# Two-layer attention encoder: the transposed blocks of P change places inside SBUF, and the products with v come later

## The chip, the core and the metric

The kernel runs on one core of a Trainium2 chip. The metric is device time in microseconds (us). The engines are TensorE (PE; PEld is its weight load), VectorE (DVE), ScalarE (ACT), GpSimd (POOL) and SyncE (SP), which here issues almost every DMA; DMAs that one engine issues go out in its program's order.

## The reference

Two layers on 512 tokens of width 1024, in float32. Layer A is dilated sliding-window attention (three dilations, merged by their softmax denominators), layer B is neighbourhood attention on an 8 x 64 grid.

```python
def reference(x, ...):
    for i in range(DEPTH):                      # DEPTH = 2
        hn = rms_norm(x, norm_gain[i])
        y = mixer_a(...) if i % 2 == 0 else mixer_b(...)
        x = x + y

def mixer_a(hn, w_in, w_out, q_gain, k_gain, t5_bias):
    qkv, gate = split(hn @ w_in)                # q, k, v for 3 dilations, 16 heads of 64
    for g, (window, dilation) in enumerate(DILATED_PAIRS):
        q, k = rms_norm(q, q_gain[g]), rms_norm(k, k_gain[g])
        o, lse = dilated_group_attention(q, k, v, bias, dilation, reach)
    y = sum(softmax(lses) * outs) * silu(gate)
    return y @ w_out

def mixer_b(hn, w_in, w_out, q_gain, k_gain, rpb):
    q, k, v, gate = split(hn @ w_in, 4)
    q, k = rms_norm(q, q_gain) * HEAD_DIM ** -0.5, rms_norm(k, k_gain)
    p = softmax(q k^T + bias)                   # 8 rows x 16 columns of neighbours
    y = (p v) * silu(gate)
    return y @ w_out
```

## The kernel before

Heads go in pairs: `NHC` = 8 pairs per layer, called heads below. Two generators run against each other and make one program for TensorE, in whose order it runs. `main` holds the dense products: for each head of layer A a projection of 512 columns to `rawk` (raw k and v), one to `rawq` (raw q and k), one to v of the first dilation (`vt`) and one to the gate; for each head of layer B one of 384 columns to `raw` (q, k, v) and one to the gate. A projection to raw takes 8 steps of 12 matmuls, the gate and `vt` 8 steps of 3, because a float32 product is made of three: `wh` with `hn_h`, `wl` with `hn_h` and `wh` with `hn_l` (a weight and an input are each split into a high and a low part).

`side` holds the attention of a head: its norm, transposes of raw q and k on TensorE (`tp`), two pairs of score tiles (`log`), softmax, the transposes of P and the products `o` of P with v (`weigh`), and `put_y`, which multiplies `o` with the gate and splits the result into `y_h` and `y_l` for the output product. After each piece of `main` the function `run` asks whether the next piece of `side` is due. A `yield` of a number in `side` lets so many ns of modelled TensorE work go by; `yield "wait", stamp, n` counts n from the moment when a stamp was set. So the numbers in the diff move pieces of `side` along TensorE's program, and no engine waits for them by time. TensorE's order is kept as it is written; the other engines' orders come from a scheduler.

P is transposed in two steps. VectorE turns each 32x32 block in place (`put`, L615, into tile `tr`); then the blocks have to change places between four groups of 32 partitions. `out` (L617) does that by writing `tr` to DRAM (`td`, L620) and reading it back in four pieces of 32 partitions (L622, into tile `pt`). A batch is one such exchange: two per head in layer A (run 512, 1 MB), one in layer B (run 448, 0.9 MB), for seven of the eight heads; the last head of a layer transposes P on TensorE. There is one `tr` and one `pt`. In layer A `o` follows 19 us of modelled work after the second batch; in layer B, `o` of a head is held in `pending` and made 10 us of work after the next head's projection to raw.

Weights come through SP's queue too, in loads of 512 or 384 KB (`wraw`, L174, three buffers); ScalarE casts them to `wh`, and VectorE or GpSimd makes `wl`, four steps ahead of TensorE. With the raw loads they run some ten steps ahead. Accumulators of projections (`acc`) use four PSUM banks in turn, `tp`, `log` and `o` four others. `gt` and `eg` of the gate have two buffers each. `head_norm` makes the norm's scale `rs`, on VectorE for `rawq` and by a chain of 14 small instructions on GpSimd for `rawk` and layer B's `raw`, and L271 applies it on VectorE.

Of the kernel before, what the change touches and what calls it, by code (L numbers as in the profile page):

```python
# [12 lines left out]
F32 = mybir.dt.float32  # L13
# [8 lines left out]
P = 128  # L22
# [3 lines left out]
NHC = 8  # L26
# [15 lines left out]
def tile_hybrid_encoder(  # L42
# [13 lines left out]
    nc = tc.nc  # L56
# [5 lines left out]
    wk = ctx.enter_context(tc.tile_pool(name="wk", bufs=2))  # L62
    ps_acc = ctx.enter_context(tc.tile_pool(name="ps_acc", bufs=4, space=PSUM))
    ps_side = ctx.enter_context(tc.tile_pool(name="ps_side", bufs=4, space=PSUM))
    dr = ctx.enter_context(tc.tile_pool(name="dr", bufs=1, space=DRAM))
# [326 lines left out]
        nc.sync.dma_start(lb_d, lb)  # L392

    st = {}

    def project_qk(n, ns, key, hc, guard, first=False, **kw):

        box = []

        def evac(i, acc):  # L400
            if not box:
                q = key == "rawq"
                box.append(wk.tile([P, 4, n], F32, tag="rawq" if q else "rawk", name=key, bufs=1 if q else 2))
                box.append(wk.tile([P, 32], F32, tag="ss", name="ss"))
            raw, ss = box
            if first:
                nc.scalar.copy(raw[:, i, :], acc[:, :n])
                return
            nc.scalar.activation(raw[:, i, :], acc[:, :n], AF.Copy, scale=rs_n[:, i : i + 1])  # L409
            squares(raw, ss, i, ns)  # L410

        tile_of = lambda hn: lambda k, i: hn[:, k, P * i : P * (i + 1)]
        yield from project(tile_of(hn_h), tile_of(hn_l), n, evac, guard, **kw)
        raw, ss = box
        if first:
            st["first"] = raw, ss
            return
        normed(raw, ss, ns, key, hc)
# [46 lines left out]
    def k_a(hc):  # L465
        yield "wait", ("rawk", hc), 10000 if hc else 12500
        k12 = wk.tile([P, 2, 512], F32, tag="k12", name="k12", bufs=1)
        raw = st.pop(("rawk", hc))
        for g in range(2):
            tp = transpose4(raw, g * P)  # L470
            nc.vector.tensor_scalar(k12[:, g, :], tp, gk[:, g + 1 : g + 2], None, op0=ALU.mult)
            yield
        st["k12", hc] = k12, raw
        stamp["k12", hc] = 0
# [129 lines left out]
    class turner:  # L604
# [11 lines left out]

        def out(self, dst):  # L617
            run = self.run
            d = dr.tile([P, 4 * run], F32, tag="td", name="td", bufs=2)
            nc.sync.dma_start(d, self.t)  # L620
            for b in range(4):
                nc.sync.dma_start(  # L622
                    dst[32 * b : 32 * b + 32, :].rearrange("p (a x) -> p a x", a=4),
                    bass.AP(d.tensor, d.offset + run * b, [[4 * run, 32], [128 * run, 4], [1, run]]),
                )

    def attn_a(hc):
        e0, e12 = st.pop(("e", hc))
# [2 lines left out]
        pts = []  # L631
# [77 lines left out]
        def weigh():  # L709
            o = bank("o")  # L710
            mms = []
            for g in range(2):
                for j in range(4):
                    c = 256 + P * g
                    mms.append((
                        lambda t_, j=j: sb(t_, 32 * j, [[256, 2], [P, 2], [1, 32]]),
                        lambda hs, j=j, c=c: v12[:, j, c + hs.start : c + hs.stop],
                        lambda hd, g=g, j=j: sb(pts[0], at(0, j, hd, 2 + g), [[2048, 2], [128, 2], [1, 32]]),
                    ))
            for i in range(4):  # L720
                (t0, i0), (t1, i1) = ((i - 1, 1), (i, 0)) if i else ((0, 0), (3, 1))
                mms.append((
                    lambda t_, d=P * t0, n=P * (t1 - t0): sb(t_, d, [[n, 2], [32, 4], [1, 32]]),
                    lambda hs, i=i: v0[hc % 2][:, i, hs],
                    lambda hd, t0=t0, i0=i0, n=at(t1, 0, 0, i1) - at(t0, 0, 0, i0): sb(
                        pts[0], at(t0, 0, hd, i0), [[n, 2], [512, 4], [1, 32]]
                    ),
                ))
            side_by_side(o, mms)
            return o  # L730

        if hc < NHC - 1:
            for u in range(2):
                yield 2500 if u == 0 else 8000
                turned = turner(512)
                for hd, t, pr in scores(u):
                    turned.put(pr, 512, 256 * hd + 128 * (t % 2))
                turned.out(pts[0][:, 2048 * u : 2048 * u + 2048])
            yield 19000
        else:  # L740
            for u in range(2):
                yield 1200
                held = scores(u)
                yield 3200
                for args in held:
                    turn_p(*args)
                    yield
            yield from v_a(hc)
            stamp["ya", "turned"] = 0
        o = weigh()  # L750
        if hc == NHC - 2:
            gap[0] = cycle((500, 500, 700))
            yield "wait", ("gate", hc), 1500
        put_y(hc, o, True, hc == NHC - 1)
        yield

    def run(main, side):

# [29 lines left out]
    gap = [cycle((1200,))]  # L788
# [71 lines left out]
        nc.scalar.activation(eg, gt, AF.Tanh, scale=0.5)  # L860
        gated(hc, gt, eg)

    pending = []

    def side_b(hc):
        if hc:
            yield "wait", ("raw", hc), 10000
            pending.pop()()
            yield 2500 if hc < NHC - 1 else 1000
        else:  # L870
            yield "wait", ("raw", hc), 12000
        raw = st.pop(("raw", hc))
        e = st.pop(("e", hc))
        qh = wk.tile([P, 512], F32R, tag="q0h", name="qh", bufs=1)
# [6 lines left out]
        for src, h, l in (  # L881
# [1 line left out]
            (edge_rc(tp), edge_q(qh), edge_q(ql)),  # L883
        ):
            nc.vector.tensor_sub(l, src, h.bitcast(F32))
        yield 2500
        tp = transpose4(raw, P)
        put_k([(kh, kl, tp)], 3)
        stamp["qk", hc] = 0
        yield 1750  # L890
        pts = []

        at = lambda a, hd, i: 448 * a + 224 * hd + 32 * i

        def scores(u):
            if u == 0:
                pts.append(wk.tile([P, 4096], F32, tag="pt", name="pt", bufs=1))
            lgs = [bank("log") for _ in range(2)]
            for b in (2 * u, 2 * u + 1):
                if b < 3:  # L900
                    m = lambda t_, hs: t_[hs, P * b : P * b + 256]
                else:
                    m = lambda t_, hs: sb(t_[hs], 0, [[384, 2], [1, P]])
                qs = slice(P * b, P * b + P)
                o = 256 * (b % 2)
                mm3_heads(
                    [lg[:, o : o + 256] for lg in lgs],
                    lambda hs: qh[hs, qs], lambda hs: ql[hs, qs], lambda hs: m(kh, hs), lambda hs: m(kl, hs), True,
                )
            return [(hd, u, softmax(hd, u, lgs[hd])) for hd in range(2)]  # L910
# [59 lines left out]
        for u in range(2):  # L970
            held += scores(u)
            yield 1200 if u == 0 else 2400
        if hc < NHC - 1:
            turned = turner(448)
            for hd, u, pr in held:
                turned.put(pr, 512 if u == 0 else 384, 224 * hd + 128 * u)
            turned.out(pts[0][:, :1792])
            pending.append(lambda: put_y(hc, weigh(), False, False))
            return
# [20 lines left out]
    def side():  # L1000
        for k in range(KT):
            norm(0, k, x_all[:, k, :])
            if k:
                square_a(k - 1)
            stamp["na", k] = 0
            yield 1000
        square_a(KT - 1)
        for k in range(1, KT):
            yield 1300
            nc.vector.tensor_add(x_all[:, 0, :], x_all[:, 0, :], x_all[:, k, :])  # L1010
        yield 1500
        row_scale(row_sums(x_all[:, 0, :]))
        st["y_h"] = big.tile([P, KT, S], F32R, tag="y", name="y_h")
        yield 2500
        bias_lines()
        st["e", 0] = bias_a(0)
        yield 2500
        scales_a()
        first_out()
        stamp["rs", "a"] = 0  # L1020
        for hc in range(NHC):
            if hc < NHC - 1:
                yield from chain(k_a(hc), q_a(hc), v_a(hc), attn_a(hc))
                if hc == 2:
                    bias_rows()
            else:
                yield from chain(q_a(hc), k_a(hc), attn_a(hc))
        yield from residual(xg)
        stamp["ya", KT - 1, "y"] = 0
        for f in range(KT):  # L1030
            yield "wait", ("x", f), 2500
            square_b(f)
        yield 1500
        row_scale(row_sums(st.pop("ssq")))
        yield 5000
        nc.scalar.copy(rs_all, spread())
        stamp["rs", "b"] = 0
        for hc in range(NHC):
            yield from side_b(hc)
            if hc + 2 < NHC:  # L1040
                st["e", hc + 2] = bias_b(hc + 2)
        yield from residual(xm_d)
        stamp["yb", KT - 1, "y"] = 0

    run(main(), side())


# [88 lines left out]
```

## Time and profile before

| what | before |
|---|---|
| time, median of three runs | 1015.43 us (1013.43 to 1016.85) |
| the profiled execution | 1015.75 us, span 1014.0 us |
| TensorE busy, mean granted clock | 891.6 us (88%), 0.938 |
| VectorE, ScalarE, GpSimd busy | 505.6 us (50%), 423.7 us (42%), 300.0 us (30%) |
| DMA | 130.48 MB, 129 GB/s over the span |
| HBM read, written | 103.73 MB, 25.75 MB |

The span is that of the core from its first to its last instruction; the execution's own time is measured around it. Busy shares are means over stages with different limits, so an engine far under 100% can still be waited for in one place.

### The profile page before, as it was taken

The page shows a single profiled execution, that of the slowest core. Times are in us where ns is not written, and L with a number is a line of the kernel's source. Part 1 is how long each engine was busy: PE and PEld are TensorE (multiplying, and loading weights), DVE is VectorE, ACT ScalarE, POOL GpSimd, SP SyncE. Part 2 cuts the span into 40 slices and gives each one's busy share as a digit, 9 for nine tenths or more (in the row PEclk, how much of TensorE's full clock was granted, in tenths as well). Part 3 has the DMA queues.
Part 4 walks back from the last instruction along what each step waited for, and adds up shares of the span by engine and source line. Part 5 has one row for each costly group of instructions (what it writes and reads, how often), then busy time and mean ns, then how long its engine had stood idle before and what let it go on. Part 6 is the DMA issues. An engine that isn't in the chain of part 4 may idle for free.

```text
span 1014.0 us, 15414 instructions
## 1 busy us (share of the span) xinstructions
PE 891.6 (88%) x5629; PEld 739.1 (73%) x5629; DVE 505.6 (50%) x1324; ACT 423.7 (42%) x888; POOL 300.0 (30%) x500
## 2 busy tenths in 40 slices
PE   9999799799799899899799899999769588596698
PEld 7787678587678678677687777889658577585476
DVE  6365265366355456366366554546354353362442
ACT  6436235236234425335235444535245253352451
POOL 2342233232341331332332411133332232241311
PEclk9999899999899999999899899999898798797899
DMA  6344613714622723714713613622451442424314
GB/s 231 95 140 140 201 63 126 215 63 140 200 81 96 209 98 118 224 63 127 215 63 128 200 48 97 214 91 78 149 150 38 140 142 61 141 91 126 117 52 177
DMA packets 51787, 130.48 MB, mean 129 GB/s; under 512 B 5504, under 2 KB 20288, under 8 KB 49920
## 3 DMA queue, kind: packets, MB, share of 16 engines
q1 hardware_dynamic: 51424, 129.49, 40.7%
q8 instruction: 44, 0.72, 0.3%
q14 instruction: 31, 0.25, 0.1%
q10 hardware_dynamic: 288, 0.01, 0.0%
HBM read 103.73 MB, written 25.75 MB: 128 GB/s over the span
## 4 chain that ended last, share of the span: by engine, by line
PE 56%; DMA 18%; DVE 12%; ACT 8%; issue 3%; SPq 2%; POOL 1%; ACTq 0%; DVEq 0%; POOLq 0%
PE acc L205 42%; DMA td<-tr 10%; DMA pt<-td 7%; PE o L205 7%; PE tp L209 4%; PE log L205 3%; ACT p L542 2%; SPq L622 2%; DVE wl L130 2%; ACT p L934 2%; DVE tr L615 1%; DVE rawq L271 1%; ACT wh L126 1%; ACT rawk L409 1%; ACT p L698 1%
## 5 line engine op out<-in xcount | busy, mean ns | idle before, releaser
L205 PE MATMUL acc<-wh,hn_h 128*128 128x512 f32 (+1 forms) x768 | 301.6, 393 | 7.0 <-ACT rawk L409 2.1
L126 ACT CAST wh<-wraw 128x512 fp32r<-128x512 f32 (+1 forms) x276 | 161.6, 586 | 309.4 <-PE acc L205 268.2
L205 PE MATMUL acc<-wl,hn_h 128*128 128x512 f32 (+1 forms) x768 | 289.0, 376 | 0.4 <-DVE wl L130 0.4
L205 PE MATMUL acc<-wh,hn_l 128*128 128x512 f32 (+1 forms) x768 | 288.7, 376 | 0.0
L130 POOL TENSOR_TENSOR wl<-wraw,wh 128x512 fp32r<-128x512 f32 (+1 forms) x110 | 138.1, 1255 | 407.9 <-ACT wh L126 368.6
L130 DVE TENSOR_TENSOR wl<-wraw,wh 128x512 fp32r<-128x512 f32 (+1 forms) x166 | 114.2, 688 | 150.2 <-ACT wh L126 145.9
L205 PEld LDWEIGHTS acc<-wh,hn_h 128*128 128x128 f32 x768 | 147.0, 191 | 41.7 <-issue 8.7
L205 PEld LDWEIGHTS acc<-wh,hn_l 128*128 128x128 f32 x768 | 146.6, 191 | 21.4
L205 PEld LDWEIGHTS acc<-wl,hn_h 128*128 128x128 f32 x768 | 147.1, 192 | 18.9 <-DVE wl L130 0.9
L205 PE MATMUL o<-pt,raw 128*64 128x64 f32 (+2 forms) x192 | 24.5, 436 | 66.5 <-DMA pt<-td 66.3
L205 PE MATMUL acc<-hn_h,wh 128*128 128x512 f32 x192 | 76.5, 399 | 0.1
L565 DVE SCALAR_TENSOR_TENSOR gt<-gt,o 128x512 f32<-128x512 f32 x15 | 10.3, 688 | 132.9 <-PE o L205 132.8
L205 PE MATMUL acc<-hn_h,wl 128*128 128x512 f32 x192 | 75.1, 391 | 0.0
L205 PE MATMUL acc<-hn_l,wh 128*128 128x512 f32 x192 | 75.0, 390 | 0.0
L542 ACT ACTIVATE p<-p,mn 128x512 f32<-128x512 f32 (+3 forms) x128 | 70.8, 588 | 1.2 <-DVE mn L541 1.2
L205 PEld LDWEIGHTS o<-pt,raw 128*64 128x64 f32 x192 | 17.3, 214 | 73.5 <-issue 63.2
L698 ACT ACTIVATE p<-p,mn 128x512 f32<-128x512 f32 (+1 forms) x64 | 44.9, 702 | 50.3 <-DVE mn L687 50.3
L205 PE MATMUL o<-pt,rawk 128*64 128x128 f32 x256 | 27.3, 399 | 39.3 <-DMA pt<-td 28.2
L256 POOL TENSOR_TENSOR sq<-rawq 128x512 f32<-128x512 f32 x32 | 33.9, 1072 | 92.1 <-ACT rawq L409 91.4
L615 DVE STREAM_TRANSPOSE tr<-p 128x512 f32<-128x512 f32 (+1 forms) x84 | 55.8, 682 | 9.1 <-ACT p L542 8.5
L257 DVE TENSOR_REDUCE ss<-sq 128x4 f32<-128x256 f32 (+1 forms) x96 | 47.9, 500 | 23.3 <-POOL sq L256 22.9
L205 PEld LDWEIGHTS o<-pt,rawk 128*64 128x64 f32 x256 | 24.7, 213 | 42.5 <-issue 42.5
(137 smaller groups left out, 1253.5 us busy)
## 6 DMA issues: line engine op xcount, KB each, us to landing
wraw<-in_w SPq DMA_DIRECT2D x95, 512.0 KB
wraw<-in_w SPq DMA_DIRECT2D x38, 384.0 KB
td<-tr SPq DMA_DIRECT2D x14, 1024.0 KB
pt<-td SPq DMA_DIRECT2D x56, 256.0 KB
td<-tr SPq DMA_DIRECT2D x7, 896.0 KB
pt<-td SPq DMA_DIRECT2D x28, 224.0 KB
e<-l_d SPq DMA_DIRECT2D x32, 112.0 KB
e<-l_d SPq DMA_DIRECT2D x16, 128.0 KB
```

The costliest lines, as they stand in the source:

```text
L126: nc.scalar.copy(h, raw)
L130: eng.tensor_sub(l, raw, h.bitcast(F32))
L205: nc.tensor.matmul(o, l, r, **kw)
L209: nc.tensor.transpose(o, i, ident)
L256: nc.gpsimd.tensor_mul(sq, raw[:, i, : ns * 64], raw[:, i, : ns * 64])
L257: nc.vector.tensor_reduce(ss[:, i * ns : (i + 1) * ns], sq.rearrange("p (a b) -> p a b", b=64), axis=AX.X, op=ALU.add)
L542: nc.scalar.activation(pr, pr, AF.Copy, scale=mn[:, 3:4])
L565: nc.vector.scalar_tensor_tensor(gt, gt, 0.5, o, op0=ALU.mult, op1=ALU.mult)
L615: nc.vector.transpose(dst, src[:, :n].rearrange("p (i b k) -> p i b k", b=4, k=32))
L622: nc.sync.dma_start(dst[32 * b : 32 * b + 32, :].rearrange("p (a x) -> p a x", a=4), bass.AP(d.tensor, d.offset + run * b, [[4 * run, 32], ...
L698: nc.scalar.activation(row, row, AF.Exp, bias=mn[:, 1:2], scale=-1.0, accum_out=mn[:, 2:3])
L934: nc.scalar.activation(pr[:, o : o + n], pr[:, o : o + n], AF.Exp, bias=mn[:, 0:1], scale=-1.0, accum_out=mn[:, 2:3])
```

## The change

`out` no longer goes through DRAM: 16 DMAs copy block (a, b) of `tr` straight to its place in `pt`, 32 partitions by `run` columns each. In layer A the products with v are held in `pending` and made during the next head, 24 us of modelled work after its projection to `rawk` (in the last head after the transposes of raw q); the second pair of scores comes 12 us of work after the first instead of 8. In layer B `o` of a head is made after the next head's two pairs of scores, not ahead of its transposes. Raw k and v of layer A and raw q, k, v of layer B share one tile `rk` now, in two halves (layer A) or three thirds (layer B); before, `rawk` had two buffers.

```diff
--- before.py
+++ after.py
@@ -392,6 +392,7 @@
         nc.sync.dma_start(lb_d, lb)
 
     st = {}
+    rk = wk.tile([P, 4608], F32, tag="rawk", name="rawk", bufs=1)
 
     def project_qk(n, ns, key, hc, guard, first=False, **kw):
 
@@ -400,7 +401,11 @@
         def evac(i, acc):
             if not box:
                 q = key == "rawq"
-                box.append(wk.tile([P, 4, n], F32, tag="rawq" if q else "rawk", name=key, bufs=1 if q else 2))
+                if q:
+                    box.append(wk.tile([P, 4, n], F32, tag="rawq", name=key, bufs=1))
+                else:
+                    o = 4 * n * (hc % (2 if n == 512 else 3))
+                    box.append(rk[:, o : o + 4 * n].rearrange("p (i c) -> p i c", i=4))
                 box.append(wk.tile([P, 32], F32, tag="ss", name="ss"))
             raw, ss = box
             if first:
@@ -616,13 +621,13 @@
 
         def out(self, dst):
             run = self.run
-            d = dr.tile([P, 4 * run], F32, tag="td", name="td", bufs=2)
-            nc.sync.dma_start(d, self.t)
-            for b in range(4):
-                nc.sync.dma_start(
-                    dst[32 * b : 32 * b + 32, :].rearrange("p (a x) -> p a x", a=4),
-                    bass.AP(d.tensor, d.offset + run * b, [[4 * run, 32], [128 * run, 4], [1, run]]),
-                )
+            for i in range(4):
+                for a in range(4):
+                    b = (a + i) % 4
+                    nc.sync.dma_start(
+                        dst[32 * b : 32 * b + 32, run * a : run * a + run],
+                        self.t[32 * a : 32 * a + 32, run * b : run * b + run],
+                    )
 
     def attn_a(hc):
         e0, e12 = st.pop(("e", hc))
@@ -731,12 +736,12 @@
 
         if hc < NHC - 1:
             for u in range(2):
-                yield 2500 if u == 0 else 8000
+                yield 2500 if u == 0 else 12000
                 turned = turner(512)
                 for hd, t, pr in scores(u):
                     turned.put(pr, 512, 256 * hd + 128 * (t % 2))
                 turned.out(pts[0][:, 2048 * u : 2048 * u + 2048])
-            yield 19000
+            pending.append(lambda: put_y(hc, weigh(), True, False))
         else:
             for u in range(2):
                 yield 1200
@@ -747,12 +752,10 @@
                     yield
             yield from v_a(hc)
             stamp["ya", "turned"] = 0
-        o = weigh()
-        if hc == NHC - 2:
-            gap[0] = cycle((500, 500, 700))
-            yield "wait", ("gate", hc), 1500
-        put_y(hc, o, True, hc == NHC - 1)
-        yield
+            put_y(hc, weigh(), True, True)
+            yield
+
+    pending = []
 
     def run(main, side):
 
@@ -860,15 +863,8 @@
         nc.scalar.activation(eg, gt, AF.Tanh, scale=0.5)
         gated(hc, gt, eg)
 
-    pending = []
-
     def side_b(hc):
-        if hc:
-            yield "wait", ("raw", hc), 10000
-            pending.pop()()
-            yield 2500 if hc < NHC - 1 else 1000
-        else:
-            yield "wait", ("raw", hc), 12000
+        yield "wait", ("raw", hc), 12000 if hc < NHC - 1 else 11000
         raw = st.pop(("raw", hc))
         e = st.pop(("e", hc))
         qh = wk.tile([P, 512], F32R, tag="q0h", name="qh", bufs=1)
@@ -883,18 +879,16 @@
             (edge_rc(tp), edge_q(qh), edge_q(ql)),
         ):
             nc.vector.tensor_sub(l, src, h.bitcast(F32))
-        yield 2500
+        yield 2500 if hc < NHC - 1 else 2000
         tp = transpose4(raw, P)
         put_k([(kh, kl, tp)], 3)
         stamp["qk", hc] = 0
-        yield 1750
+        yield 1750 if hc < NHC - 1 else 1250
         pts = []
 
         at = lambda a, hd, i: 448 * a + 224 * hd + 32 * i
 
         def scores(u):
-            if u == 0:
-                pts.append(wk.tile([P, 4096], F32, tag="pt", name="pt", bufs=1))
             lgs = [bank("log") for _ in range(2)]
             for b in (2 * u, 2 * u + 1):
                 if b < 3:
@@ -970,6 +964,11 @@
         for u in range(2):
             held += scores(u)
             yield 1200 if u == 0 else 2400
+        if hc:
+            yield 2500 if hc < NHC - 1 else 500
+            pending.pop()()
+            yield
+        pts.append(wk.tile([P, 4096], F32, tag="pt", name="pt", bufs=1))
         if hc < NHC - 1:
             turned = turner(448)
             for hd, u, pr in held:
@@ -1020,11 +1019,21 @@
         stamp["rs", "a"] = 0
         for hc in range(NHC):
             if hc < NHC - 1:
-                yield from chain(k_a(hc), q_a(hc), v_a(hc), attn_a(hc))
+                yield from k_a(hc)
+                if hc:
+                    yield "wait", ("rawk", hc), 24000
+                    pending.pop()()
+                    yield
+                yield from chain(q_a(hc), v_a(hc), attn_a(hc))
                 if hc == 2:
                     bias_rows()
             else:
-                yield from chain(q_a(hc), k_a(hc), attn_a(hc))
+                yield from q_a(hc)
+                gap[0] = cycle((500, 500, 700))
+                yield "wait", ("gate", hc - 1), 1500
+                pending.pop()()
+                yield
+                yield from chain(k_a(hc), attn_a(hc))
         yield from residual(xg)
         stamp["ya", KT - 1, "y"] = 0
         for f in range(KT):
```

The order on SP in layer A, head 4, before: a batch is a write to DRAM, a weight load and four reads, with the bias loads (`e`) of a later head between the two batches. After it the same place with the change.

```order
L622 DMA pt<-td 32x4x512 x4
L174 DMA wraw<-in_w 128x1024 x7
L620 DMA td<-tr 128x2048
L174 DMA wraw<-in_w 128x1024
L622 DMA pt<-td 32x4x512 x4
L578 DMA e_4183<-l_d 128x1x256 x2
L583 DMA e_4184<-l_d 128x1x224 x2
L174 DMA wraw<-in_w 128x1024
L583 DMA e_4184<-l_d 128x1x224 x2
L620 DMA td<-tr 128x2048
```

```order
L627 DMA pt<-tr 32x512 x16
L174 DMA wraw<-in_w 128x1024 x8
L627 DMA pt<-tr 32x512 x16
L174 DMA wraw<-in_w 128x1024 x2
L583 DMA e_4290<-l_d 128x1x256
L588 DMA e_4291<-l_d 128x1x224 x2
L583 DMA e_4290<-l_d 128x1x256
L588 DMA e_4291<-l_d 128x1x224 x2
L627 DMA pt<-tr 32x512 x16
```

A batch is now one row of 16 copies. The bias loads and two weight loads still stand between the first batch and the second, and the eight weight loads of the rest of the head stand behind the second.

The order on TensorE in layer B, around the products `o` of one head (their `raw` operand is called `rawk` after the change), before and with the change:

```order
L205 MATMUL acc<-wh,hn_l 128x384
L205 MATMUL o<-pt,raw 64x128 x2
L205 MATMUL o<-pt,raw 64x64 x2
L205 MATMUL o<-pt,raw 64x256 x2
L205 MATMUL o<-pt,raw 64x64 x2
L205 MATMUL o<-pt,raw 64x256 x2
L205 MATMUL o<-pt,raw 64x128 x2
L205 MATMUL acc<-wh,hn_h 128x384
```

```order
L205 MATMUL acc<-hn_h,wl 128x512
L205 MATMUL o<-pt,rawk 64x128 x2
L205 MATMUL o<-pt,rawk 64x64 x2
L205 MATMUL o<-pt,rawk 64x256 x2
L205 MATMUL o<-pt,rawk 64x64 x2
L205 MATMUL o<-pt,rawk 64x256 x2
L205 MATMUL o<-pt,rawk 64x128 x2
L205 MATMUL acc<-hn_h,wh 128x512
```

Before, `o` stands in the middle of the next head's projection to raw, 18 products ahead of the transposes of its raw q. Now it stands inside a gate product, after 9 of its 24 matmuls for heads from the third on, and 36 products follow that gate product before transposes of raw. In layer A, 90 products lie between the last score and `o` before, and 111 with two transposes now.

The order on GpSimd in the same place, from the end of one norm's chain on, before (the steps of the chain for `rs` are L107 to L119), and with the change, where the rows show the middle of the chain:

```order
L118 TENSOR_SCALAR na<-na 128x16
L130 TENSOR_TENSOR wl<-wraw,wh 128x384
L119 TENSOR_TENSOR rs<-rs,na 128x16
L130 TENSOR_TENSOR wl<-wraw,wh 128x384
L570 TENSOR_TENSOR y_l<-gt,y_h 128x384
L570 TENSOR_TENSOR y_l<-gt,y_h 128x2x64
L130 TENSOR_TENSOR wl<-wraw,wh 128x512
L256 TENSOR_TENSOR sq<-raw 128x256 x4
```

```order
L118 TENSOR_SCALAR na<-na 128x16
L119 TENSOR_TENSOR rs<-rs,na 128x16
L575 TENSOR_TENSOR y_l<-gt,y_h 128x384
L112 TENSOR_TENSOR na<-rs 128x16
L575 TENSOR_TENSOR y_l<-gt,y_h 128x2x64
L117 TENSOR_TENSOR na<-na,nv 128x16
```

Both `y_l` of a head have moved from behind a finished norm into the middle of the next head's norm.

## Rows read from the trace of the kernel before

**Rows 1.** Span and mean granted TensorE clock of the core

```profile
core 0: 1014.0 us, clock 0.938
```

**Rows 2.** Groups of TensorE by line, with idle time before them and its releasers

```profile
L205 PE MATMUL o<-pt,rawk 128*64 128x128 f32 x256 | 27.3, 399 | 39.3 <-DMA pt<-td 28.2 <-DMA wraw<-in_w 6.6 <-issue 4.5
L205 PE MATMUL o<-pt,raw 128*64 128x64 f32 (+2 forms) x192 | 24.5, 436 | 66.5 <-DMA pt<-td 66.3 <-DVE pt L946 0.2
```

**Rows 3.** Chain that ended last, layer A: start us, length us, what

```profile
122.94 5.32 PE o L205 x48
...
170.74 1.98 PE log L205 x75
172.72 11.13 PE acc L205 x48
184.79 8.48 DMA td<-tr
194.61 6.13 DMA pt<-td
200.93 5.58 PE o L205 x48
...
578.39 6.28 PE o L205 x48
...
625.71 3.62 PE o L205 x48
```

**Rows 4.** Chain that ended last, layer B

```profile
730.71 3.13 PE acc L205 x18
...
765.76 4.39 PE acc L205 x18
...
789.43 5.47 DMA td<-tr
796.27 6.37 DMA pt<-td
802.77 3.10 PE o L205 x24
```

**Rows 5.** Busy time by window: PE, PEld, DVE, ACT, POOL, then granted clock

```profile
762.00:765.00 3.00, 2.50 (x20) 1.99 (x22) 0.00 (x0) 0.00 (x0) 0.00 (x0) 0.50 0.00 0
```

**Rows 6.** Tile pt: duration ns of an issue, min/median/max

```profile
L622 SPq DMA_DIRECT2D pt<-td x84: 302/424/2209, 96.2 to 955.4; - x84
```

**Rows 7.** VectorE in order of time, layer A: start us, length us

```profile
179.58 1.88 DVE L615 STREAM_TRANSPOSE tr<-p 128x512 f32<-128x512 f32 x3
```

**Rows 8.** TensorE in order of time, layer B

```profile
780.97 0.39 PE L205 MATMUL acc<-hn_h,wh 128*128 128x512 f32 x1
...
788.13 0.41 PE L205 MATMUL acc<-wh,hn_h 128*128 128x384 f32 x1
```

**Rows 9.** VectorE in order of time, layer B

```profile
786.74 1.25 DVE L857 TENSOR_TENSOR gt<-acc,rs_all 128x384 f32<-128x384 f32 x2
...
788.84 0.56 DVE L615 STREAM_TRANSPOSE tr<-p 128x384 f32<-128x384 f32 x1
...
791.93 1.43 DVE L271 TENSOR_TENSOR raw<-raw,rs 128x256 f32<-128x256 f32 x4 [1.86 <-POOL rs L119]
```

**Rows 10.** ScalarE in order of time, layer B

```profile
767.47 1.20 ACT L569 CAST y_h<-gt 128x384 fp32r<-128x384 f32 x2
```

**Rows 11.** GpSimd in order of time, layer B

```profile
768.62 1.71 POOL L570 TENSOR_TENSOR y_l<-gt,y_h 128x384 fp32r<-128x384 f32 x2
```

**Rows 12.** TensorE in order of time, layer A

```profile
300.91 0.48 PE L209 MATMUL tp<-ident,rawq 128*128 128x128 f32 x1 [1.35 <-DVE rawq L271]
...
363.26 0.40 PE L205 MATMUL acc<-hn_h,wh 128*128 128x512 f32 x1
...
377.77 0.49 PE L209 MATMUL tp<-ident,rawq 128*128 128x128 f32 x3
```

**Rows 13.** VectorE in order of time, layer A, head 4

```profile
372.85 3.47 DVE L271 TENSOR_TENSOR rawq<-rawq,rs 128x512 f32<-128x512 f32 x4
```

## The prediction

> **What bounds the kernel now.** I read four views, in this order. The core's span and clock come first: 1014.0 us at a mean granted clock of 0.938 [rows 1]; the profiled execution took 1015.75 us, 0.3 above the median of the three runs, so sums made against it carry over. Next the groups of TensorE by line. TensorE is busy for 88% of the span, and nearly all of its idle time stands before one kind of instruction: the products `o` of the transposed P (tile `pt`) with v. 39.3 us stand before those of layer A and 66.5 before those of layer B, and the releaser is the DMA `pt<-td` [rows 2] (where "issue" or a weight load is named, PE had nothing else to wait for: the copies of `pt` were still under way). That is seven waits in each layer, 105.8 us.
>
> The chain of waits shows what a head waits for. In layer A [rows 3]: the second pair of score tiles (`log`) ends at 172.7, then TensorE has products of the projection, while `td<-tr` runs from 184.8 for 8.5 us, `pt<-td` from 194.6 for 6.1, and `o` starts at 200.9. In layer B [rows 4]: `td` from 789.4, `pt` from 796.3, `o` at 802.8. So 13.3 to 16.1 us lie between finished 32x32 transposes and the product, all of it a write to DRAM and a read back.
>
> Last, the clock. The first products behind a wait run slowly: the windows give 0.50 granted in 762 to 765 [rows 5], 1.2 instead of 2.4 GHz. The `o` of layer A takes 5.32 to 6.28 us after a wait (first and last of seven; they add up to 40.1) and 3.62 in the last head, which has no wait before it [rows 3]. In layer B it takes 3.1 behind the wait, and the 18 products after it 4.39 where the same 18 take 3.13 in dense work [rows 4].
>
> **The change, part by part.** *DRAM round trip replaced by 16 block copies.* Per batch, one `td` and four `pt` DMAs go, 16 of 32 x run come, all on SP's queue. No row shows a copy within SBUF. An issue of `pt<-td` costs SP 302 ns at least, 424 in the median [rows 6]; 16 of them 4.8 to 6.8 us. From above: the four pieces of 256 KB needed 6.1 to 6.4 us, 1.6 each if they went one after the other [rows 3, 4]; if a block of 64 KB cost the same, a batch would take 25.6. I take 6.8 for issuing and 2.2 for the last to land, 9 us, because the issue rate is the nearest row to a quarter-sized piece. The Trainium skill speaks against this part: "DMA: Bandwidth & Descriptors", section "Rules for kernel authors", wants small transfers coalesced and calls those under 64 KB mostly overhead, and its section on the anatomy of a DMA fits 2.0 us plus bytes over 436 GB/s. By that, 2.15 us a block, a batch of blocks in turn would take 34 us and the sum would come to about 1,270; no run here shows a block yet, and the page also says that fixed costs overlap when transfers are issued early.
>
> *Products with v later.* Layer A: between the last score of a head and its `o` there stood 90 products of 512 columns, now 111 and two transposes; at 11.13/48 = 0.232 us each [rows 3] that is 26.5 us. The transposes of P end 8.7 us after the scores (181.46 against 172.72 [rows 7, 3]), SP has 3.3 us of bias loads still to issue before them (184.79), and 9 us of copies bring `pt` to 21 us. The wait is covered with 5 us over. Layer B: `o` moves behind the scores of the next head. The transposes end at 789.40, 8.4 us after the gate product's start [rows 8, 9]; that start now lies 15 products of 0.174 us further from the scores, so they end 5.8 after it and `pt` lands at 15. `o` comes a whole head later: 96 products at 0.174, 24 at 0.232, and some 5 us of `o`, scores and transposes, about 27 us. Covered by 12 us.
>
> So the waits go, and with them the slow clock: 39.3 + 66.5 idle; 40.1 - 7 x 3.62 = 14.7 for `o` in A; at least 1 each, 7, for `o` in B (half speed would say 1.6); and about 1.2 in four heads of B for the products behind, 5. Together 132.5, or 883.
>
> *What is late next.* `o` brings its own followers along: VectorE's `gt`, ScalarE's `y_h` (1.20 us in B [rows 10]), GpSimd's `y_l` (1.71 [rows 11]). Before, they ran right after a wait, when nobody needed them. In layer B they now fall into the norm of the next raw q, k. As the order shows, both `y_l` stand inside GpSimd's chain for `rs`, and VectorE's `gt` of the next gate (which takes the same one of two buffers, so it waits for `y_l`) frees the accumulator that the fourth block of the next projection needs. Counted from the gate product's start: `o` ends at 9 x 0.232 + 2.2 = 4.3, `gt` at 5, `y_h` at 6.3, `y_l` at 8 to 9.1 (with the chain's steps around it), the next `gt` (1.25 [rows 9]) at 9.3 to 10.3. The fourth block is reached at 5.6 + 2.2 + 1.6 = 9.4. Before it was reached at 7.2, 0.14 after `gt` had ended [rows 8, 9]. A new wait of 0 to 1.5; I take 1.3, for six heads 8. The transposes of raw stand at 13.8; their scale ended 12.4 after the start before (793.36 against 780.97 [rows 9, 8]), now 1.7 later: the same wait, not a second one. The last head of B has fewer products in that place, 2 more.
>
> In layer A the transposes of `rawq` follow the end of its projection by 14.5 us (377.77 against 363.26), and the scale was ready 13.1 after it [rows 12, 13]. They now follow after 45 products and an `o`, 14.1; on VectorE `gt` comes in between, 0.7. A wait of 0 to 1.4 per head (one head already shows 1.35 [rows 12]), 0.5 taken, six heads 3. Waits pull the clock down for a moment; 2 for that. Together 15, up to 45 if every one is 3.
>
> *Other edits.* Raw v in three thirds of one tile costs nothing: scale and transposes go by region, and a third is rewritten only a head after `o` has read it. SP is held for 6.8 us by a batch, before for 8.5 by the wait on `td` and 1.7 by the pieces; weight loads behind it had that delay already. Without this cover each batch would hold up the casts that feed TensorE by what the copies exceed 9 us.
>
> **Sum:** 1015.75 - 132.5 + 15 = 898 us.
>
> **The rivals.** (1) *Cover complete.* None of the new waits shows, because the chains of VectorE and GpSimd start earlier in a dense head: 876 to 888. For it: the scale was 1 us early in both layers. Against: `y_l` adds 1.7 exactly there. (2) *The norm becomes the bound.* The other engines had slack only because TensorE stood still; each head then waits 3 us and runs slowly behind it: 883 + 45 or more, 910 to 935. For it: 0.14 us of slack before the fourth block. Against: by the table both VectorE and ScalarE are busy for half of the span or less. (3) *Weights.* The next weight load stands behind 16 issues; if an issue costs 0.8, it comes 6 us later, 3 to 6 us per head of B are lost: 920 to 940. Against: the loads run some ten steps ahead. (4) *Slower:* a block costs like a piece of four times its size, and the batch takes its place as the wait. In layer A two batches and the transposes between them must fit between the first scores and `o`: 57 products and the second scores (15.2) plus 26.5 us, less 8.7 until the first transposes are done, 2.6 for the second transposes and 3.3 for the bias loads, 27 us for 32 blocks. Above 0.85 us a block each 0.1 costs 3.2 us per head, 22 over the layer; above about 1.4 the change is slower than before. At 1.6 layer A loses 168, and layer B, where a batch may take 23 us, 2.5 per head: some 1,080. The skill's fixed cost per DMA, above, is this rival's rule. Against: four issues of 0.42 and a wait of 6 us for a whole 1 MB say that transfers overlap. (5) *The change doesn't do what it says:* `o` still waits for `pt` as long as before, say for a copy that is queued behind weights: 1010 to 1018.
>
> **How the numbers follow.** Forecast (890 to 909) 0.52; (1) 0.16; (2) 0.20; (3) 0.05; (4) 0.05; (5) 0.02. The predicted time is 898. From 878 to 928 it takes in the forecast, most of (1) and (2), some of (3). About 0.3%, 3 us, is what a measurement of this kernel can tell from no change. Faster: the first four cases, 0.93; same: 0.02; slower: (4), 0.05.
>
> **What would show it.** Right: the idle time before `o` under 5 us in all, `o` of layer A at 3.6 us in every head, 8 to 10 us from the first block's issue to the last landing, and short waits (0.5 to 1.5 us) before the fourth block of B's projections and before transposes of raw q. Wrong: blocks more than 0.5 us apart on SP; idle before weights' products; waits of 3 us on VectorE or GpSimd in each head; a granted clock still at 0.50 behind them.

## The result and the profile after

The changed kernel takes 918.22 us (median of four runs, 915.51 to 923.95) against 1015.72 before: ratio 0.905, 95% interval 0.900 to 0.910. The profiled execution is the fastest of the four, 915.51 us with a span of 913.7. 898 was predicted, 878 to 928 as the range.

The span, and who TensorE (PE) waits for in the changed kernel (us in total, times, longest us):

```profile
core 0: 913.7 us, clock 0.981
```

```profile
PE acc L205 <- ACT rawq L414: 23.4, 5, 5.1
PE tp L209 <- DVE rawq L271: 3.6, 7, 1.1
PE o L205 <- DMA pt<-tr: 3.6, 2, 3.4
PE acc L205 <- DVE gt L860: 2.3, 1, 2.3
```

The fourteen waits of [rows 2], 105.8 us, are down to the 3.6 us of the first head. The largest wait is new: five times 4.1 to 5.1 us, all in layer A, for ScalarE's evacuation of `rawq` (its copy of finished accumulators out of PSUM). No step of the prediction has it.

What one head takes, by windows from its first scores to those of the next (busy time of PE, PEld, DVE, ACT, POOL; then the granted clock, the DMA share and GB/s). First before, then after; the first row is the fourth head of layer A, the second a head in the middle of layer B, and the third of after is a stretch of the first:

```profile
315.80:389.80 74.00, 68.08 (x471) 55.02 (x470) 40.26 (x98) 30.73 (x57) 22.91 (x37) 0.98 0.44 138
815.20:854.90 39.70, 29.92 (x177) 26.59 (x176) 16.57 (x54) 16.59 (x44) 12.31 (x25) 0.87 0.35 110
```

```profile
298.00:372.60 74.60, 69.42 (x471) 55.70 (x470) 38.28 (x98) 31.03 (x58) 22.47 (x36) 0.95 0.35 109
757.80:785.60 27.80, 27.69 (x177) 24.55 (x176) 18.13 (x55) 16.71 (x44) 12.50 (x24) 1.00 0.40 127
...
343.00:349.00 6.00, 6.00 (x15) 4.65 (x15) 1.76 (x3) 2.67 (x5) 5.16 (x5) 0.50 0.17 63
```

A head of layer B went from 39.7 to 27.8 us, dense and at full clock. A head in the middle of layer A did not get faster at all, though its wait before `o` is gone; it idles 5 us in another place and has a lower clock than before. From the first scores of the first head to those of the last, layer A gained 24.4 us (517.6 to 493.2) and layer B 80.5 (272.4 to 191.8). Of layer A's gain 22 us lie in three of its heads, the first (8.5), the third (6.5) and the seventh (6.9); the four others changed by 1.2 or less.

The chain shows the new wait in that head of layer A, from 300 to 353 us (start us, length us, what), and the products behind the other four waits:

```profile
194.72 5.61 PE acc L205 x15
...
268.72 6.12 PE acc L205 x15
...
300.09 11.13 PE acc L205 x48
...
323.15 9.01 DMA e<-l_d
332.18 0.51 SPq L627
...
337.86 3.64 DMA wraw<-in_w
341.60 0.62 ACT wh L126
342.22 0.60 ACT rawq L414
342.86 6.55 PE acc L205 x15
349.41 3.62 PE o L205 x47
...
417.06 5.30 PE acc L205 x15
...
489.80 6.48 PE acc L205 x15
```

Read backwards: PE waits for an accumulator that `rawq` must leave; in ScalarE's order a cast `wh` stands ahead of that; the cast waits for a weight load; and the weight load stands on SyncE behind the second batch of copies. SyncE (SP) and ScalarE in order of time in that stretch:

```profile
306.67 0.33 SPq L174 DMA_DIRECT2D wraw<-in_w  x1
307.26 10.87 SPq L627 DMA_DIRECT2D pt<-tr  x16
318.24 1.02 SPq L174 DMA_DIRECT2D wraw<-in_w  x2
...
321.80 2.59 SPq L588 DMA_DIRECT2D e<-l_d  x2
324.49 13.26 SPq L627 DMA_DIRECT2D pt<-tr  x16
337.86 1.50 SPq L174 DMA_DIRECT2D wraw<-in_w  x3
```

```profile
321.38 0.61 ACT L126 CAST wh<-wraw 128x512 fp32r<-128x512 f32 x1
...
332.76 0.62 ACT L126 CAST wh<-wraw 128x512 fp32r<-128x512 f32 x1 [2.06 <-PE acc L205]
341.60 0.62 ACT L126 CAST wh<-wraw 128x512 fp32r<-128x512 f32 x1 [8.21 <-DMA wraw<-in_w]
342.12 2.42 ACT L414 ACTIVATE rawq<-acc,rs_n 128x512 f32<-128x512 f32 x4
```

For 30.6 us (307.26 to 337.86) SyncE issues 32 copies, six bias loads and two weight loads. ScalarE was idle: the 2.4 us of evacuation could have run at 338. Both engines keep their order. The copies of the second batch also wait for the slow bias loads: in the trace SyncE's DMAs count their landing on eight counters in turn, so a DMA waits for the one issued eight before it, and the chain has the eighth copy start when an `e` has landed (332.18 after 323.15 + 9.01). Three copies lose 1.7 us so; another 1.6 lie in the issue of the batch's first copy, for which the trace gives no reason.

The clock falls behind each of the five waits: the last window above lies behind the third of them. The 15 products between a wait and `o` are the rows `acc` x15 of the chain. The five are 30.1 us, where 15 products at the 0.232 us of layer A [rows 3] take 3.5: 12.7 us lost, at a mean granted clock of 0.53 to 0.68 in these stretches (0.50, 1.2 GHz, in the window above). With 23.4 of idle time that is 36 us, 7 for each of the five heads.

### The profile page after: what moved, and what is told of

The parts are those of the page before. It is cut to its first block, busy times and chain, and to the rows that moved or that the text cites. A ratio compares the mean times of both kernels' runs of the same rounds, so it can differ in the third digit from the quotient of the medians.

```text
span 913.7 us, 15704 instructions
## 1 busy us (share of the span) xinstructions
PE 870.3 (95%) x5629; PEld 718.0 (79%) x5629; DVE 505.9 (55%) x1324; ACT 425.6 (47%) x888; POOL 299.0 (33%) x500
## 4 chain that ended last, share of the span: by engine, by line
PE 67%; DMA 9%; SPq 7%; DVE 6%; ACT 4%; issue 2%; POOL 2%; ACTq 0%; DVEq 0%
PE acc L205 55%; DMA e<-l_d 6%; SPq L627 6%; PE o L205 5%; PE tp L209 3%; PE log L205 3%; DMA wraw<-in_w 2%; DVE rawq L271 2%; ACT rawk L414 2%; SPq L588 1%; ACT wh L126 1%; DVE wl L130 1%; ACT p L547 1%; DMA pt<-tr 1%; DVE hn_l L355 1%
## 5 line engine op out<-in xcount | busy, mean ns | idle before, releaser
L205 PE MATMUL acc<-wh,hn_h 128*128 128x512 f32 (+1 forms) x768 | 295.3, 384 | 4.6 <-DVE gt L860 2.3
L205 PE MATMUL acc<-wl,hn_h 128*128 128x512 f32 (+1 forms) x768 | 285.4, 372 | 0.7 <-DVE wl L130 0.7
L205 PE MATMUL acc<-hn_h,wh 128*128 128x512 f32 x192 | 83.7, 436 | 23.7 <-ACT rawq L414 23.4
L205 PE MATMUL acc<-hn_l,wh 128*128 128x512 f32 x192 | 79.6, 415 | 0.0
L205 PE MATMUL acc<-hn_h,wl 128*128 128x512 f32 x192 | 79.1, 412 | 0.0
L205 PEld LDWEIGHTS acc<-hn_h,wh 128*128 128x128 f32 x192 | 39.2, 204 | 39.5 <-ACT rawq L414 25.8
L256 POOL TENSOR_TENSOR sq<-rawk 128x256 f32<-128x256 f32 x64 | 40.6, 642 | 51.9 <-ACT rawk L414 43.7
L205 PE MATMUL acc<-y_h,wh 128*128 128x512 f32 x128 | 51.9, 406 | 0.0
L205 PE MATMUL acc<-y_h,wl 128*128 128x512 f32 x128 | 50.0, 391 | 0.0
L205 PE MATMUL acc<-y_l,wh 128*128 128x512 f32 x128 | 50.0, 390 | 0.0
```

Source lines behind the costliest of these rows:

```text
L205: nc.tensor.matmul(o, l, r, **kw)
L256: nc.gpsimd.tensor_mul(sq, raw[:, i, : ns * 64], raw[:, i, : ns * 64])
```

## The experiments

Theory 1: the later products made the gain, the copies did not. Theory 2: the new waits of layer A come from weights that stand on SyncE behind two batches and the loads between them. Rivals: the copies are what helps; ScalarE's own work makes `rawq` late; DMA bandwidth. Ratios are against the kernel before, with 95% intervals. Layers and heads of other kernels are told as above, from scores to scores.

**e1_copies_only.** The kernel before, with `out` as in the change and nothing else.

> The kernel before with the 16 block copies alone: the products with v, the scores and the buffers stay as before. Theory 1 (the later products made the gain; a batch of copies is about as long as the DRAM trip): the waits before `o` stay, each shorter by about 1 us (from the end of the transposes to `o` 16.1 us in layer A and 13.3 in layer B before; 13.3 + 2 and 10.1 + 2 with the copies as the changed kernel's SyncE rows show them): 1000 us, 985 to 1015. Rival (the copies made the gain): at least half of the 97 us is there, below 965.

985.78 us, 0.971 (0.967 to 0.975). The waits before `o` stay, 20.9 us in layer A and 59.1 in layer B for 39.3 and 66.5. So the copies alone do not make the gain, but they save more than I thought, 31 us. This kernel has the same batches and bias loads on SyncE as the changed one, and yet:

```profile
PE o L205 <- DMA pt<-tr: 71.2, 16, 9.7
...
PE acc L205 <- ACT rawq L409: 2.0, 2, 1.4
```

A weight is late here too: in the fourth head of layer A a cast waits 6.1 us for one and starts at 349.84. But it falls into the time of the wait and of `o`, in which TensorE asks for no weights, and costs next to nothing. The wait that the change removes had hidden the next one.

**e2_later_only.** The changed kernel, with the trip through DRAM put back:

```diff
-            for i in range(4):
-                for a in range(4):
-                    ...
+            d = dr.tile([P, 4 * run], F32, tag="td", name="td", bufs=2)
+            nc.sync.dma_start(d, self.t)
+            for b in range(4):
+                ...
```

> The changed kernel with the trip through DRAM put back (one write, four reads): only the later products and the places of raw v are left of the change. Theory 1: the later place covers 16 us as well as 13 to 15, so nearly the whole gain stays, and a batch keeps SyncE shorter (8.5 us of wait and 1.7 of issues against 13), so that the new waits of layer A shrink: 890 to 915 us. Rival (the copies are needed): waits before `o` come back, above 950.

886.98 us, 0.873 (0.871 to 0.875): 31 us faster than the whole change, and below the range that I gave. The five waits for ScalarE are gone. The window of the same head of layer A:

```profile
287.60:353.60 66.00, 66.00 (x469) 53.71 (x468) 39.41 (x98) 31.36 (x58) 22.85 (x36) 1.00 0.49 155
```

SyncE there, from the second batch on:

```profile
313.53 0.34 SPq L625 DMA_DIRECT2D td<-tr  x1
314.14 1.51 SPq L174 DMA_DIRECT2D wraw<-in_w  x1
321.31 1.74 SPq L627 DMA_DIRECT2D pt<-td  x4
323.17 22.02 SPq L174 DMA_DIRECT2D wraw<-in_w  x5
```

It takes 66.0 us instead of 74.6, with more bytes moved (155 GB/s against 109), so it was not bandwidth; a head of layer B takes 27.8 us as with the copies. The five DMAs keep SyncE 2.1 us here (2.7 in the first batch) and for one wait, and weight loads go out within it and after it: the first one behind the second batch leaves 9.6 us after `td` was issued, against 13.4 behind the copies' start.

**e3_bias_off_sp.** The bias loads issued on ScalarE: in `bias_a`, twice, `nc.sync.dma_start` becomes `nc.scalar.dma_start`.

> The changed kernel with the six bias loads of each head of layer A issued on ScalarE instead of SyncE. Theory 2 (the new waits of 4.1 to 5.1 us in layer A come from a weight load that stands on SyncE behind both batches and the bias loads): the second batch takes 10.5 us instead of 13.3 and starts when its transposes end, the weight behind it lands 3.2 us earlier, the five waits shrink to 1 to 2 each: 890 us, 880 to 905. Rival (the evacuation of rawq is late for ScalarE's own work, softmax among it): the same 918 or more, since ScalarE gets 3 us of issues more per head.

920.84 us, 0.907 (0.904 to 0.910): no gain, which by my numbers speaks for the rival. The trace says otherwise. ScalarE (ACTq are its DMA issues):

```profile
325.89 1.47 ACTq L588 DMA_DIRECT2D e<-l_d  x1
...
327.40 2.03 ACTq L588 DMA_DIRECT2D e<-l_d  x1
329.48 1.34 ACT L547 ACTIVATE p<-p,mn 128x512 f32<-128x512 f32 x2 [2.69 <-issue]
```

The issues hold up the softmax behind them by 2.7 us, the transposes end late, and the second batch starts at 331.58, 19.0 us behind the first (312.59) where the changed kernel has 17.2. Times of two runs can only be compared so, from a place in the same head; the 7 us in what was expected of e5 leave that out. TensorE now waits 10.1 us for `rawq`, in two places, 7.2 for `vt` and 12.6 ahead of transposes. The wait was moved, not taken away; the run decides nothing between the theories.

**e4_deeper_weights.** Four buffers `wraw` for three, and the loads one further ahead:

```diff
-            raw = wp.tile([P, 1024], F32, tag="wraw", name="wraw", bufs=3)
+            raw = wp.tile([P, 1024], F32, tag="wraw", name="wraw", bufs=4)
...
-            if len(queue) > 2:
+            if len(queue) > 3:
```

> The changed kernel with four buffers for weight loads instead of three, and the loads one further ahead. Everything else on SyncE stays, the batches and the bias loads too. Theory 2: the load behind the second batch is needed 28 products (6.5 us) later, the five waits of 4.1 to 5.1 us go, and the slow clock behind them (12 us in all): 880 us, 872 to 895. Rival (DMA bandwidth, or ScalarE's own work): the waits stay, 910 to 920.

895.02 us, 0.880 (0.877 to 0.883), at the upper end. All five waits are gone, with SyncE's batches as long as before (10.65 and 13.27 us in that head). In ScalarE's order the same cast still stands ahead of the evacuation, but its weight is there and it waits for TensorE alone; a weight is late only behind the evacuation:

```profile
334.15 0.62 ACT L126 CAST wh<-wraw 128x512 fp32r<-128x512 f32 x1 [2.14 <-PE acc L205]
334.78 2.73 ACT L414 ACTIVATE rawq<-acc,rs_n 128x512 f32<-128x512 f32 x4
...
340.14 0.62 ACT L126 CAST wh<-wraw 128x512 fp32r<-128x512 f32 x1 [2.12 <-DMA wraw<-in_w]
```

Three heads of layer A take 66.0 us now, and one 78.8, that in which the bias rows of layer B are loaded (e11 has more on it). ScalarE's casts and evacuations in that head stand in the same order and only the loads come earlier, which settles theory 2 against ScalarE's own work; against bandwidth speaks e2, with more bytes in less time.

**e5_bias_on_pool.** As e3, but with `nc.gpsimd.dma_start`.

> The changed kernel with the six bias loads of each head of layer A issued on GpSimd: on ScalarE (the run before) two of them waited 1.5 and 2.0 us and held up the softmax, so the second batch began 7 us later than it could. Theory 2 (what holds up the weights is the time for which SyncE is kept by two batches and the loads between them): SyncE is free of the loads, the second batch starts when its transposes end, takes 10.5 us instead of 13.3, and the weight behind it comes some 3 us earlier; waits of 1 to 2 us stay: 895 us, 885 to 908. Rival (bias loads don't matter, wherever they are): 914 to 922.

908.26 us, 0.893 (0.888 to 0.898), just above the range. The waits for ScalarE are gone and another takes their place:

```profile
PE tp L209 <- DVE rawk L271: 16.8, 7, 7.0
```

In the same fourth head the second batch starts on SyncE at 321.70 and takes 11.14 us, and the weight leaves at 332.96, 27.4 us behind the start of the first batch (305.52) instead of 30.6, as theory 2 has it. But the loads now stand inside GpSimd's chain for `rs`, and the first scores of all come at 91.1 us instead of 80.0. The middle heads take 68.7 to 70.5 us for 73.0 to 74.6.

**e6_halves_b.** Each block of layer B in two copies of half its columns, 32 per batch.

> The changed kernel with each block of layer B moved in two copies of half its columns, 32 per batch, the same bytes; layer A as it is. If a copy costs SyncE its issue (0.63 us whatever its size), a batch takes 20 us, `pt` lands 28 us after the gate product's start where `o` stands at 27, and the weights behind it come 10 us later: waits of 1 to 8 us per head of layer B, 925 to 985. Rival (a copy costs by its bytes): a batch stays at 10 us and the time at 918.

953.84 us, 0.938 (0.933 to 0.944). A batch on SyncE, and PE's waits that are new:

```profile
759.66 20.89 SPq L629 DMA_DIRECT2D pt<-tr  x32
```

```profile
PE acc L205 <- ACT wh L126: 21.7, 7, 5.3
PE o L205 <- DMA pt<-tr: 4.5, 3, 3.3
```

A batch of the same bytes takes 20.7 to 21.8 us instead of 10.0 to 10.8: here the copies cost SyncE by their number, not by their bytes. And the price is paid as in layer A: 21.7 us for weights, with next to nothing before `o`. A head takes about 33 us instead of 27.8.

**e7_copies_on_pool.** All 16 copies issued by GpSimd.

> The changed kernel with all block copies issued on GpSimd instead of SyncE. Theory 2: SyncE's queue is free of them, weights come early, and the five waits of layer A for ScalarE go; but GpSimd is kept instead, some 10 us per batch or more, in which its `wl` casts and its part of the norm wait: 885 to 925, with TensorE's waits now behind GpSimd. Rival (the waits of layer A have nothing to do with SyncE's queue): the same five waits, 918 or more.

1065.13 us, 1.047 (1.041 to 1.054): the waits for ScalarE are gone, as theory 2 says, but I had the price of it far too low.

```profile
PE tp L209 <- DVE rawk L271: 120.8, 13, 18.5
```

The issue itself is not dearer here (498 ns in the median, on SyncE 589), but it stands between the casts, squares and norm of GpSimd, and the norm of raw k comes up to 18.5 us late.

**e8_later_deeper.** e2 with the four `wraw` buffers of e4.

> The products later, the trip through DRAM put back, and four buffers for weight loads, one load further ahead: the two edits that gave 887 and 895 by themselves. Theory 2: with the trip through DRAM the weights are in time already in all heads but the one in which three more loads for layer B stand on SyncE (that head takes 7.5 us longer than the 66.0 of its neighbours), so the deeper queue can give back at most these 7.5: 880 to 888. Rival (weights are still tight everywhere): below 878.

887.48 us, 0.873 (0.868 to 0.878): the same as e2. The head that takes 73.5 us in e2 is hardly better (72.6), so late weights, the reason that I gave for it, were not its cause.

**e9_copies_b_only.** Through DRAM where `run == 512`, that is layer A; copies in layer B.

> The changed kernel with the trip through DRAM in layer A only; layer B keeps its copies. Theory 2: layer B takes 27.8 us a head either way, and all that the copies cost stands in layer A: 887 us, 882 to 893, as with the trip in both layers. Rival (the copies cost in layer B too, or do good there): 5 us or more away from 887.

887.40 us, 0.875 (0.872 to 0.878), as predicted. In layer B copies and trip are worth the same once `o` comes late; all that the copies cost stands in layer A.

**e10_second_dram.** Through DRAM for the second batch of a head of layer A only (`turned.out` with `u == 1`).

> The changed kernel with the trip through DRAM for the second batch of each head of layer A only; the first keeps its 16 copies, and layer B keeps its own. Theory 2: a weight load can go out while SyncE waits for the write of `td`, the next one comes some 3 us earlier than behind 16 copies (1.7 us of issues and 8 of waiting, against 13.3), so that the five waits of 4.1 to 5.1 us shrink to 0 to 1: 890 us, 884 to 900. Rival (the first batch matters as much): 900 to 910.

897.41 us, 0.885 (0.882 to 0.888). The five waits for ScalarE are gone, and three heads take 66.0 to 66.3 us: the second batch is the one that counts there. Most of what the profiled execution (892.80 us) lacks to e2 stands in the first head, 73.6 us for 67.8, in a longer wait before its `o` (3.0 us in e2). Its `td` goes out at 108.84 us, right behind the 16 copies of the first batch and the bias loads, in e2 at 105.06:

```profile
PE o L205 <- DMA pt<-td: 7.7, 1, 7.7
```

**e11_later_rows.** e2 with the loads of layer B's bias rows in another place:

```diff
                     pending.pop()()
+                    if hc == 3:
+                        bias_rows()
...
-                if hc == 2:
-                    bias_rows()
```

> The products later with the trip through DRAM, and the three loads and stores of layer B's bias rows moved from behind the second batch of the third head to behind `o` of the next. Their cause, by the trace: GpSimd waits 13.4 us for the load `rp`, which stands on SyncE behind `pt`, and the squares of raw q behind it make the transposes late, so this head takes 73.5 us where others take 66.0. If that is right, it falls to 66 to 68: 880 us, 877 to 884, the fastest of all. Rival (the loads only move the wait to the next head): 885 to 890.

879.84 us, 0.867 (0.865 to 0.869): the fastest of all, 134 us below the kernel before. That head falls from 73.5 to 66.0 us. It was GpSimd that waited for a load on SyncE, not the weights; this wait of e2 is 1.7 us in e11:

```profile
POOL rp L387 <- DMA rp<-in_rpb: 13.4, 1, 13.4
```

## Why the prediction was right, and where it was not

*The waits before `o`.* Right. 35.7 of 39.3 us went in layer A and all 66.5 in layer B; `o` of layer A takes 3.62 us in every head but the first, as forecast. (One reading was off, without effect on the sum: in layer A 19.5 us lie between the finished transposes, 181.46 [rows 7], and `o`; the 16.1 are counted from the issue of `td`.)

*Slow clock in the old places.* Counted too low. Without the new waits the changed kernel would stand at 883 by the prediction's sum; with 23.4 + 12.7 (the new wait and the slow products behind it), 3.6 before the first `o`, 1.6 and 3.4 (the two parts on what is late next, below) added that makes 928, and 915.5 was measured. By layers: layer A gave back 65.7 us (24.4 net and 41.3 of new losses) where 54 were counted, layer B 83.9 for 78.5, and the rest of the program lost 4.6. TensorE's busy time fell by 21.3 us (891.6 to 870.3) although 12.7 of slow products are new; that is 34.0 for 26.7 counted, so more than half of these 12 us is products that ran slowly before. `o` of layer B is 4 of them, with

```profile
739.81 1.69 PE o L205 x24
```

now for 3.08 to 3.26 before: 10.7 us in seven heads, where "at least 1 each, 7" was counted. The rest I did not trace.

*Price of a batch.* "0.42" us an issue was mis-sized. The changed kernel's issues:

```profile
L627 SPq DMA_DIRECT2D pt<-tr x336: 507/589/2407, 89.3 to 863.6; - x168
```

0.59 in the median and 0.63 from one to the next; a batch takes 10.0 to 11.1 us, 12.9 to 14.0 behind bias loads, and its last copy about 2 to land. That is 12 us and more where "8 to 10" were to show the prediction right; blocks over 0.5 us apart and a clock at 0.50 behind waits, two of its signs of being wrong, both came. The choice of the nearest row was right in kind (e6: the number of issues sets it) and a third too low. The Trainium skill, "DMA: Bandwidth & Descriptors", section "Rules for kernel authors", said to coalesce, and that under 64 KB one pays mostly overhead. The time by the Trainium skill's fixed cost (34 us a batch) is far off: 16 copies are issued and landed in 12 to 13 us where no bias load stands before them, so their fixed costs overlap; and that fit is one of DMAs that GpSimd issues, while SyncE issues these. By direction the rule was right in layer A (e2 against the change: 31 us), whose blocks are 64 KB; those of layer B, 56 KB and so below that bound of the Trainium skill, cost nothing (e9). What is paid in layer A is paid on the issuing queue.

*SyncE's hold.* This is the step that failed: "weight loads behind it had that delay already", so no cost was set. Three things were wrong with it. The hold grew to 13.3 us in the second batch. In the trip a weight load goes out while SyncE waits for `td`; behind 16 copies it can't. And the delay that the weights "had already" fell into PE's wait for `pt`, which the change removes (e1 against the change). The consequence, 36 us in layer A, took the gain there; e4 gives 23 us of it back with one more buffer. The prediction had a rival of this kind, (3), but looked for it in layer B, at a higher price per issue, and gave it 0.05. "The loads run some ten steps ahead" was the argument against it; but four of the ten are casts already made, and the next cast stands ahead of `rawq` on ScalarE. The three loads up to 319.26 feed six casts (321.38 to 332.76), six steps of 12 products at 0.232, 16.7 us; the next load goes out 18.6 us behind them and takes 3.6 to land. By this count it is 5.5 us late; the wait measured 4.7.

*What is late next, layer B.* The mechanism is as drawn, the size was not. VectorE, then PE, in one head:

```profile
773.27 1.22 DVE L860 TENSOR_TENSOR gt<-acc,rs_all 128x384 f32<-128x384 f32 x2 [2.16 <-POOL y_l L575]
```

```profile
765.29 0.50 PE L205 MATMUL acc<-hn_h,wh 128*128 128x512 f32 x1
...
774.18 0.34 PE L205 MATMUL acc<-wh,hn_l 128*128 128x384 f32 x1
774.63 0.41 PE L205 MATMUL acc<-wh,hn_h 128*128 128x384 f32 x1
```

`gt` waits for `y_l` and ends 9.2 us after the gate product's start (765.29), where 9.3 to 10.3 were worked out; the fourth block starts at 9.34, 0.28 later than at the pace of 0.174. So "8" us for six heads were about 3.4, one wait of 2.3 and 0.28 in four heads, and the transposes waited 0.2 in all.

*What is late next, layer A.* "3" us for the transposes of `rawq`: 3.6, of which 2.0 had been there before:

```profile
PE tp L209 <- DVE rawq L271: 2.0, 3, 1.3
```

In all, the total came out near by luck: 39.7 us that no step had (23.4 + 12.7 in layer A, 3.6 before the first `o`) stand against 12 of gains counted too low and 10 of the 15 for new waits and their clock that did not come. The mechanism held in layer B; in layer A it left out the wait that sets the time there.

## What to carry to other kernels

A wait on the engine that sets the time also gives every queue behind it time to catch up. Before you take it away, list what else is late by then (here: SyncE's weights) and count how many us of lead each has against the longest hold of its queue, not on average. One DMA more on a queue cost its issue here, 0.63 us for 28 KB as for 56, and delayed all that stood behind it there: count issues per batch, and see which loads can go out between them. When two edits come together, try each alone: here one was worth 130 us, and the other 31 alone, but minus 31 beside the first.

## What the runs showed of the hardware that was not expected

The issue of a copy within SBUF of 32 partitions costs 0.51 us at least, more than the 0.30 to 0.42 of one of four times its bytes from DRAM [rows 6]; halving the copies' size doubled the time of a batch (10.0 to 10.8 against 20.7 to 21.8 us). The Trainium skill, "DMA: Bandwidth & Descriptors", section "Issuing engines are not separate DMA queues", says that issuing from several engines saves only the time of issuing, usually small beside the DMA. Here it is 0.5 to 0.6 us beside some 2 until a copy has landed, and for batches of 16 it decided: moved to GpSimd (e7), 16 x 0.5 us a batch cost 147 us in all, and six loads on ScalarE (e3) cost all that they gave SyncE.
